# One shared semaphore and one wait for a last load and two partial sums, with other piece sizes in the last row

## The chip, the cores and the metric

The kernel runs on one core of a Trainium2 chip. The metric is the device time of the slowest core in microseconds (us); with one core there is only that. A profile also has a *span*, from the first instruction of the kernel to its last; the device time is longer.

The engines named in the profile are DVE (VectorE), ACT (ScalarE), POOL (GpSimd) and SP (SyncE, which issues all transfers here). SPq and DVEq are the instruction queues (sequencers) of SP and DVE.

## The reference

```python
def setup_inputs():
    batch, seq, dim = 32, 512, 1024
    return {"x": np.random.randn(batch, seq, dim).astype(np.float32)}

def reference(x):
    relu_x = np.maximum(x, 0)
    return np.sum(relu_x, axis=-1).astype(np.float32)
```

67 MB are read, 64 KB are written. Each of the 16,384 sums takes 1024 numbers.

## The kernel before

The rows are laid on 128 partitions, 128 rows to a partition. Seven chunks of 16 rows a partition (8 MB each) go through three buffers; then come loads of 8, 4, 2 and 1 rows, and a last row in three pieces. On the first six chunks ScalarE applies the relu to groups of rows and VectorE sums groups of rows; `ACT_STEPS` and `DVE_STEPS` are the groups. Afterwards both engines do relu and sum in one instruction, row by row.

```python
BIG = 16
ACT_STEPS = [[7, 9], [7, 9], [4, 5, 7], [4, 5, 7], [4, 5, 7], [3, 4, 5]]
DVE_STEPS = [[7, 9], [7, 4, 5], [4, 5, 7], [4, 5, 7], [4, 5, 7], [3, 4, 5]]
TAIL = [8, 4, 2, 1]
LAST = [512, 256, 256]
# ... (chunks: a buffer is refilled when VectorE has summed all of it)
    parts = [buf[:, tb, r, 0:n0], buf[:, tb, r, n0:n1], last[:, 0 : LAST[2]]]
    for k, (lo, hi) in enumerate([(0, n0), (n0, n1), (n1, D)]):
        sp.dma_start(out=parts[k], in_=xv[-1][:, BIG - 1, lo:hi]).then_inc(
            s_in[NBIG + len(TAIL) + k], 16
        )
# ... (the summing of a chunk)
        for n in DVE_STEPS[c]:
            if ready[r + n - 1] > seen:
                seen = ready[r + n - 1]
                dve.wait_ge(s_act, seen)
            dve.tensor_reduce(
                out=res[:, c * BIG + r : c * BIG + r + n],
                in_=buf[:, c % NB, r : r + n, :], axis=X, op=ALU.add,
            ).then_inc(s_dve, 1)
            r += n
# ... (the last row)
    n = LAST[2]
    act.wait_ge(s_in[-3], 16)
    on_act(parts[0], last[:, n : n + 1]).then_inc(s_part, 1)
    dve.wait_ge(s_in[-2], 16)
    on_dve(parts[1], last[:, n + 1 : n + 2]).then_inc(s_part, 1)
    dve.wait_ge(s_part, 2)
    dve.wait_ge(s_in[-1], 16)
    on_dve(last[:, :], res[:, J - 1 : J]).then_inc(s_tdve, 1)

    sp.wait_ge(s_tdve, 1)
    sp.dma_start(out=ov[-1][:, :], in_=res[:, start[-1] : J]).then_inc(s_out, 16)
```

The last row: ScalarE sums its first piece and VectorE its middle piece, and each writes its partial sum into one of two extra columns beside the last piece. VectorE's last instruction then sums the last piece and the two extra columns together (a partial sum of relus is never negative, so the relu does not touch it). That instruction therefore needs three things: the last load, ScalarE's partial, VectorE's own partial.

## Time and profile before

| | before |
|---|---|
| device time, median of 3 runs | 161.14 us (161.12 to 161.21) |
| span of the profile | 159.8 us |
| DMA queue 1, share of 16 engines' span | 98.0% |
| DVE busy, ACT busy | 121.4 us (76%), 101.5 us (64%) |
| landing of the last load to the end of the span | some 2.1 us |

The row to start from is the third: the transfers fill the span, and the engines fit beside them.

### The profile page before, as it was taken

How to read it: one execution, taken by the hardware profiler on the slowest of the kernel's cores; microseconds unless marked ns; L12 is line 12 of the kernel's file. 1: busy time of each engine (PE TensorE's matmuls, PEld its weight loads, DVE VectorE, ACT ScalarE, POOL GpSimd, SP SyncE). 2: the span in 40 equal slices, each digit the busy share in tenths (PEclk: the TensorE clock that was granted, in tenths of full speed). 3: DMA queues.
4: the chain of work that ended last, by engine and by line, in shares of the span. 5: the costliest groups of instructions: out<-in, count | busy, mean ns of one | idle time of the engine just before them, and what ended most of it. 6: DMA issues, size and time to landing. Idle time of an engine off the chain costs nothing.

```text
span 159.8 us, 149 instructions
## 1 busy us (share of the span) xinstructions
DVE 121.4 (76%) x58; ACT 101.5 (64%) x55; POOL 0.2 (0%) x4
## 2 busy tenths in 40 slices
DVE  0000000999959999999969989699899999598995
ACT  3000059990699708996099951999339980496974
POOL 0000000000000000000000000000000000000000
DMA  9979996996997998999979969969969969899993
GB/s 377 492 323 415 492 525 263 525 525 263 525 476 312 525 427 361 525 394 394 525 312 476 525 279 509 525 263 525 525 263 525 509 279 525 353 435 390 416 404 122
DMA packets 2449, 67.18 MB, mean 421 GB/s; under 512 B 528, under 2 KB 784, under 8 KB 1168
## 3 DMA queue, kind: packets, MB, share of 16 engines
q1 hardware_dynamic: 2448, 67.18, 98.0%
q14 instruction: 1, 0.01, 0.0%
HBM read 67.11 MB, written 0.07 MB: 420 GB/s over the span
## 4 chain that ended last, share of the span: by engine, by line
DMA 68%; ACT 18%; DVE 11%; SPq 1%; issue 0%
DMA buf<-in_x_dram 68%; ACT buf L133 18%; DVE res L148 11%; SPq L95 1%; SPq L103 0%; DVE last L118 0%; DVE buf L118 0%
## 5 line engine op out<-in xcount | busy, mean ns | idle before, releaser
L148 DVE TENSOR_REDUCE res<-buf 128x7 f32<-128x7168 f32 (+4 forms) x17 | 100.1, 5923 | 33.9 <-ACT buf L133 33.9
L133 ACT ACTIVATE buf<-buf 128x7168 f32<-128x7168 f32 (+4 forms) x16 | 80.7, 5099 | 46.0 <-DMA buf<-in_x_dram 46.0
L115 ACT ACTIVATE buf<-buf 128x1024 f32<-128x1024 f32 (+1 forms) x19 | 19.0, 1001 | 9.0 <-DMA buf<-in_x_dram 8.9
L118 DVE TENSOR_SCALAR_CACHE_REDUCE buf<-buf 128x1024 f32<-128x1024 f32 (+2 forms) x19 | 20.9, 1146 | 2.8 <-DMA buf<-in_x_dram 2.7
L115 ACT ACTIVATION_READ_ACCUMULATOR buf<-buf 128x1 f32 x19 | 3.5, 187 | 0.0
L133 ACT ACT_TABLE_LOAD x1 | 1.3, 1283 | 1.3 <-PEq L209 1.3
L118 DVE DVE_READ_ACCUMULATOR buf<-buf 128x1 f32 x19 | 1.6, 83 | 0.0
L118 DVE TENSOR_SCALAR_CACHE_REDUCE last<-last 128x258 f32<-128x258 f32 x1 | 0.4, 423 | 0.0
L178 DVE TENSOR_TENSOR res<-half 128x1 f32<-128x1 f32 x1 | 0.2, 160 | 0.1
L209 POOL MEMSET const-bfloat16-1.0<- 128x1 bf16 x1 | 0.1, 102 | 0.0
L209 POOL MEMSET const-uint8-127<- 128x1 uint8 x1 | 0.1, 101 | 0.0
L209 POOL MEMSET const-float32-0.0<- 128x1 f32 x1 | 0.1, 99 | 0.2 <-issue 0.2
L209 POOL MEMSET const-float32-1.0<- 128x1 f32 x1 | 0.1, 98 | 0.0
L118 DVE DVE_READ_ACCUMULATOR last<-last 128x1 f32 x1 | 0.1, 83 | 0.0
## 6 DMA issues: line engine op xcount, KB each, us to landing
buf<-in_x_dram SPq DMA_DIRECT2D x1, 7680.0 KB, 21.4
buf<-in_x_dram SPq DMA_DIRECT2D x1, 4096.0 KB, 26.7
buf<-in_x_dram SPq DMA_DIRECT2D x1, 2048.0 KB, 31.2
buf<-in_x_dram SPq DMA_DIRECT2D x2, 512.0 KB, 18.8
buf<-in_x_dram SPq DMA_DIRECT2D x1, 1024.0 KB, 33.2
buf<-in_x_dram SPq DMA_DIRECT2D x1, 256.0 KB, 34.2
buf<-in_x_dram SPq DMA_DIRECT2D x1, 128.0 KB, 34.1
last<-in_x_dram SPq DMA_DIRECT2D x1, 128.0 KB, 33.9
```

The lines of the kernel that those rows point to most:

```text
L95: sp.dma_start(out=buf[:, tb, r : r + n, :], in_=xv[-1][:, r : r + n, :]).then_inc(s_in[NBIG + i], 16)
L115: return act.activation(t, t, AF.Relu, accum_out=acc)
L118: return dve.tensor_scalar(out=t, in0=t, scalar1=0.0, scalar2=None, op0=ALU.max, op1=ALU.add, accum_out=acc)
L133: act.activation(t, t, AF.Relu).then_inc(s_act, 1)
L148: dve.tensor_reduce(out=res[:, c * BIG + r : c * BIG + r + n], in_=buf[:, c % NB, r : r + n, :], axis=X, op=ALU.add,).then_inc(s_dve, 1)
L178: dve.tensor_tensor(out=res[:, j0 + r : j0 + r + 1], in0=half[:, 0:1], in1=half[:, 1:2], op=ALU.add)
L209: nc = _bacc.Bacc("TRN2", target_bir_lowering=False, num_devices=1)
```

## The change

The load of the last piece no longer has a semaphore of its own. It counts on the one that the two partial sums count on, and VectorE's last instruction waits once, for 16 + 2 = 18. The pieces of the last row become 512, 224, 288, to make VectorE's own partial ready sooner. And VectorE's reduction of 9 rows in the first chunk is cut into 4 and 5.

```diff
-DVE_STEPS = [[7, 9], [7, 4, 5], [4, 5, 7], [4, 5, 7], [4, 5, 7], [3, 4, 5]]
+DVE_STEPS = [[7, 4, 5], [7, 4, 5], [4, 5, 7], [4, 5, 7], [4, 5, 7], [3, 4, 5]]
 TAIL = [8, 4, 2, 1]
-LAST = [512, 256, 256]
+LAST = [512, 224, 288]
@@
-    n_in = NBIG + len(TAIL) + len(LAST)
+    n_in = NBIG + len(TAIL) + len(LAST) - 1
@@
-            s_in[NBIG + len(TAIL) + k], 16
+            s_in[NBIG + len(TAIL) + k] if k < 2 else s_part, 16
@@
-    act.wait_ge(s_in[-3], 16)
+    act.wait_ge(s_in[-2], 16)
     on_act(parts[0], last[:, n : n + 1]).then_inc(s_part, 1)
-    dve.wait_ge(s_in[-2], 16)
+    dve.wait_ge(s_in[-1], 16)
     on_dve(parts[1], last[:, n + 1 : n + 2]).then_inc(s_part, 1)
-    dve.wait_ge(s_part, 2)
-    dve.wait_ge(s_in[-1], 16)
+    dve.wait_ge(s_part, 16 + 2)
     on_dve(last[:, :], res[:, J - 1 : J]).then_inc(s_tdve, 1)
```

## The prediction

> **What bounds the kernel now.** I read the page's slices first, then busy time by stretch, the chain of waits in order of time, the groups by shape, and last the timeline of the final two microseconds.
>
> The slices (tenths of busy time in 40 parts of the span):
>
> ```profile
> DVE  0000000999959999999969989699899999598995
> ACT  3000059990699708996099951999339980496974
> DMA  9979996996997998999979969969969969899993
> ```
>
> The DMA row is full from the first slice to the last but one, while VectorE (DVE) and ScalarE (ACT) have holes. Busy time by stretch, cut where each 8 MB chunk lands, which is 0.02 us ahead of ScalarE's first step on it in the timeline (length, DVE, ACT, POOL, clock, DMA share, GB/s):
>
> ```profile
> 41.15:60.50 19.35, 17.36 (x4) 13.95 (x2) 0.00 (x0) 1.00 1.00 434
> 60.50:79.85 19.35, 19.35 (x4) 14.04 (x3) 0.00 (x0) 1.00 1.00 434
> 99.20:118.55 19.35, 17.47 (x4) 14.04 (x3) 0.00 (x0) 1.00 1.00 434
> ```
>
> ScalarE starts on the chunks at 41.17, 60.52, 79.87, 99.22 and 118.57: always 19.35 us apart, at a DMA share of 1.00 in each stretch shown, so the transfers alone set the pace until the last byte is in. What a change of waits can move is only what follows the last bytes. The end of the chain of waits (start, us, what):
>
> ```profile
> 123.29 34.06 DMA buf<-in_x_dram
> 157.35 0.02 issue
> 157.37 0.32 DVE buf L118
> 157.69 0.03 issue
> 157.72 0.09 DVE buf L118
> 157.81 0.02 issue
> 157.84 0.43 DVE last L118 x2
> ```
>
> The middle piece of the last row lands at 157.35, VectorE sums it until 157.81, and the last piece starts at 157.84, straight behind VectorE's own work. When did that last piece land? The view of the tile "last" gives:
>
> ```profile
> L103 SPq DMA_DIRECT2D last<-in_x_dram x1: 447/447/447, 123.8 to 123.8; - x1
> DMA to landing us min/median/max: 33.9/33.9/33.9
> ```
>
> The timeline has this issue at 123.78, so it landed at 123.78 + 33.9 = 157.68, give or take 0.05 for rounding. The other arm is ScalarE's, in the timeline:
>
> ```profile
> 156.99 0.63 ACT L115 ACTIVATE buf<-buf 128x512 f32<-128x512 f32 x1
> 157.37 0.42 DVE L118 TENSOR_SCALAR_CACHE_REDUCE buf<-buf 128x256 f32<-128x256 f32 x1 [0.15 <-DMA buf<-in_x_dram]
> 157.53 0.19 ACT L115 ACTIVATION_READ_ACCUMULATOR buf<-buf 128x1 f32 x1
> 157.72 0.08 DVE L118 DVE_READ_ACCUMULATOR buf<-buf 128x1 f32 x1
> 157.84 0.42 DVE L118 TENSOR_SCALAR_CACHE_REDUCE last<-last 128x258 f32<-128x258 f32 x1
> 158.29 0.34 SPq L193 DMA_DIRECT2D out_dram<-res  x1
> ```
>
> ScalarE's partial is ready at 157.53 + 0.19 = 157.72. So three things must be there before the last instruction: the load at about 157.68, ScalarE's partial at 157.72, VectorE's own at 157.81. VectorE's own comes last. The last load has about 0.13 us of slack, the ScalarE arm 0.09 us.
>
> **What the Trainium skill says.** "DMA: Bandwidth & Descriptors", section "Why a DMA increments its semaphore by 16 and not by 1", says that each of up to 16 engines posts one increment, and that a semaphore shared by two transfers in flight can pass a wait too early. Here only one transfer shares its semaphore, with two single increments, and the wait asks for 18, the sum of all; it can pass only when all three are in. No run here has shown it yet; the result's correctness will. "Perfetto Trace Analysis", section "Identifying Dependency Chains", says that an instruction that waits on several engines may get an extra semaphore instruction ahead of it. That is what the change takes away. The trace of before shows no such row; the gap at this place is 0.03 us (157.81 to 157.84), and single waits show the same: the addition of the halves starts 0.03 us after ScalarE's half (156.84 + 0.19 = 157.03 to 157.06), the final store 0.03 us after VectorE's last read (158.18 + 0.08 = 158.26 to 158.29). The same page, section "Per-instruction lifecycle", says that a VectorE window runs from execution to write acknowledgement and leaves out waits and propagation; these 0.03 us gaps agree. The DMA page, section "How a descriptor splits into AXI transactions", says that a descriptor that doesn't start on 256 bytes also fetches from the boundary below. The last piece will start at column 736, byte 2944, which is 11.5 times 256. No run here shows its cost.
>
> **The change part by part.**
>
> (1) The first chunk's reduction of 9 rows becomes 4 + 5. The groups by shape (count, busy us, mean ns, idle before):
>
> ```profile
> L148 DVE TENSOR_REDUCE res<-buf 128x5 f32<-128x5120 f32 x5 | 27.4, 5482 | 0.0
> L148 DVE TENSOR_REDUCE res<-buf 128x4 f32<-128x4096 f32 x5 | 22.1, 4416 | 2.8 <-ACT buf L133 2.8
> L148 DVE TENSOR_REDUCE res<-buf 128x9 f32<-128x9216 f32 x1 | 9.8, 9753 | 0.2 <-ACT buf L133 0.2
> ```
>
> 4416 + 5482 - 9753 = 145 ns more. Both halves wait for the same ScalarE step, so nothing starts earlier. The reduction ends at 45.69 in place of 45.54. That frees the buffer of the fourth chunk, issued now at 45.57, but the third chunk is still streaming until 60.50: some 15 us of slack. VectorE itself idles 1.83 us after it, waiting for ScalarE (timeline, at 47.38). On the path: 0.
>
> (2) Middle piece 256 to 224 columns. Per column VectorE takes (686 - 420) / 256 = 1.04 ns, from the groups 128x512 (686 ns) and 128x256 (420 ns); 32 fewer are 33 ns. The piece also lands earlier: 32 x 4 x 128 = 16 KB less; at the 364 to 434 GB/s of the traces 38 to 45 ns, call it 0.04 us. Landing 157.31, start 157.33, accumulator read done 0.44 - 0.03 = 0.41 us later at 157.74 (was 157.81).
>
> (3) Last piece 256 to 288 columns, the instruction 258 to 290: 33 ns more. All bytes together are the same, so it lands as before at 157.68; if the misaligned start costs 128 bytes on each of 128 rows, that is another 16 KB, 0.04 us: 157.72.
>
> (4) One wait for 18 in place of two waits. The gaps above say 0.03 us either way: 0, at most some 0.02.
>
> Sum: the last instruction can start 0.03 us after the latest of VectorE 157.74, ScalarE 157.72 and the load 157.68 to 157.72, so at 157.77 in place of 157.84: 0.07 earlier. It takes 0.033 longer. VectorE ends, and the store starts, 0.04 us earlier. **161.14 - 0.04 = 161.10 us.** The change is a balancing act: three arms within 0.06 us of each other in place of 0.13.
>
> **The rivals.** (a) *The load becomes the bound.* The misaligned 1152-byte rows land later than thought, say 157.80: the start is then about where it was and the longer instruction makes it 0.03 slower, 161.17. For it: the landing is known to 0.05 only and the last microsecond moves 304 to 374 GB/s, not 434. Against it: 0.13 us of slack to eat.
> (b) *The waits were worth more than the gaps show.* If the second wait hid a decode, another 0.02 to 0.03 goes: 161.07. Against it: the gap after two waits equals that after one.
> (c) *The split reduction reaches the end.* If VectorE's 0.145 us were carried through, 161.25. Against it: the idle times above, and the DMA share of 1.00 in all the stretches between.
> (d) *The build itself moves the time*, through placement or start-up, by more than any of these. The three runs of before spread over 0.09 us (161.12 to 161.21), twice my effect; only this could carry it out of the range.
>
> **Range and chances.** Mechanisms alone give 161.05 to 161.20; run spread widens it to 161.00 to 161.25, which I take for 8 in 10. Two per cent would be 3.2 us, more than everything after the last byte (157.3 to 159.8), so faster or slower by that needs the stream itself to change, and no part touches it: 0.01 each, 0.98 for within 2%.
>
> **What would show it right or wrong.** Right: chunks still 19.35 us apart; the middle piece's reduction near 387 ns and the last near 456 ns; the gap ahead of the last instruction still about 0.03 us; the store issued 0.04 us sooner relative to the middle piece's old landing. From the middle piece's landing to the last instruction's start I expect 0.46 us (157.31 to 157.77), with the chain still running through the middle piece; a longer distance, and a chain that comes from the DMA of "last", would show rival (a). A gap under 0.02 us shows (b). A longer chunk spacing, or VectorE no longer idle ahead of the second chunk's first reduction, shows (c). I am wrong on the mechanism if the end moves while these rows do not, and wrong on the whole if the stream's rate changes.

## The result, and the profile after

The changed kernel took 161.22 us (median of 6 runs, 161.11 to 161.23), the kernel before 161.15 us in the same rounds (6 runs, 160.99 to 161.21). The ratio is 1.0004 with a 95% interval of 0.9991 to 1.0017: the same.

The slices of the changed kernel's page show the transfers as full as before:

```profile
DMA  9979996996996998989979969969969969899993
```

The busy time by stretch, again cut where the chunks land (start and end of the stretch, length, DVE, ACT, POOL, clock, DMA share, GB/s):

```profile
41.19:60.54 19.35, 17.43 (x4) 13.95 (x2) 0.00 (x0) 1.00 1.00 434
99.24:118.59 19.35, 17.47 (x4) 14.04 (x3) 0.00 (x0) 1.00 1.00 434
```

The stream is untouched: 19.35 us a chunk at 434 GB/s, only the whole of it 0.04 us later in this one execution. The cut reduction stands in the timeline (start, duration, engine, what it does, in brackets the idle time before it):

```profile
35.84 9.81 DVE L148 TENSOR_REDUCE res<-buf 128x4 f32<-128x4096 f32 x2 [0.15 <-ACT buf L133]
47.42 7.62 DVE L148 TENSOR_REDUCE res<-buf 128x7 f32<-128x7168 f32 x1 [1.76 <-ACT buf L133]
```

The two take 9.81 us together (9.75 for the one of before), and VectorE still idles 1.76 us after them (1.83 before). Then the end of the chain of waits of the changed kernel (start, us, what):

```profile
122.31 34.01 DMA buf<-in_x_dram
156.32 0.02 issue
156.35 1.41 ACT buf L115 x4
157.75 0.02 issue
157.77 0.47 DVE last L118 x2
```

It no longer passes through VectorE's middle piece but through ScalarE. The timeline shows why:

```profile
157.02 0.63 ACT L115 ACTIVATE buf<-buf 128x512 f32<-128x512 f32 x1
157.31 0.39 DVE L118 TENSOR_SCALAR_CACHE_REDUCE buf<-buf 128x224 f32<-128x224 f32 x1
157.56 0.19 ACT L115 ACTIVATION_READ_ACCUMULATOR buf<-buf 128x1 f32 x1
157.62 0.08 DVE L118 DVE_READ_ACCUMULATOR buf<-buf 128x1 f32 x1
157.77 0.46 DVE L118 TENSOR_SCALAR_CACHE_REDUCE last<-last 128x290 f32<-128x290 f32 x1
158.27 0.34 SPq L192 DMA_DIRECT2D out_dram<-res  x1
```

VectorE's partial is ready at 157.62 + 0.08 = 157.70, ScalarE's at 157.56 + 0.19 = 157.75, and the last instruction starts at 157.77 (before: 157.84). The groups by shape have the two resized instructions (count, busy us, mean ns, idle before):

```profile
L118 DVE TENSOR_SCALAR_CACHE_REDUCE last<-last 128x290 f32<-128x290 f32 x1 | 0.5, 456 | 0.1
L118 DVE TENSOR_SCALAR_CACHE_REDUCE buf<-buf 128x224 f32<-128x224 f32 x1 | 0.4, 386 | 0.1
```

The middle one fell from 420 to 386 ns, the last one rose from 423 to 456. The store is issued at 158.27 in place of 158.29. With the landings to the nanosecond, as the trace's semaphore records have them:

| ready, us from the span's start | before | after |
|---|---|---|
| first piece of the last row lands | 156.969 | 156.997 |
| middle piece lands | 157.349 | 157.287 |
| last piece lands | 157.644 | 157.661 |
| ScalarE's partial | 157.715 | 157.742 |
| VectorE's partial | 157.800 | 157.705 |
| last instruction starts | 157.835 | 157.774 |
| last instruction's sum is read out (end) | 158.265 | 158.239 |
| first piece's landing to that end | 1.296 | 1.242 |

So the tail behaves as planned: measured from the landing of the first piece, it is 0.054 us shorter. None of that is seen in the time, whose runs of one kernel already spread over 0.1 to 0.2 us. The span of both profiles is 159.8 us.

### The profile page after: what moved, and what is told of

It is laid out like the page before. It is cut to its first block, busy times and chain, and to the rows that moved or that the text cites. A ratio compares the mean times of both kernels' runs of the same rounds, so it can differ in the third digit from the quotient of the medians.

```text
span 159.8 us, 149 instructions
## 1 busy us (share of the span) xinstructions
DVE 121.5 (76%) x59; ACT 101.4 (63%) x55; POOL 0.2 (0%) x4
## 4 chain that ended last, share of the span: by engine, by line
DMA 68%; ACT 18%; DVE 11%; SPq 1%; issue 0%
DMA buf<-in_x_dram 68%; ACT buf L133 18%; DVE res L148 11%; ACT buf L115 1%; SPq L95 1%; DVE last L118 0%
## 5 line engine op out<-in xcount | busy, mean ns | idle before, releaser
L148 DVE TENSOR_REDUCE res<-buf 128x4 f32<-128x4096 f32 (+3 forms) x18 | 100.1, 5601 | 33.9 <-ACT buf L133 33.9
L118 DVE TENSOR_SCALAR_CACHE_REDUCE last<-last 128x290 f32<-128x290 f32 x1 | 0.5, 456 | 0.1
```

What stands on the lines that cost most here:

```text
L118: return dve.tensor_scalar(out=t, in0=t, scalar1=0.0, scalar2=None, op0=ALU.max, op1=ALU.add, accum_out=acc)
L148: dve.tensor_reduce(out=res[:, c * BIG + r : c * BIG + r + n], in_=buf[:, c % NB, r : r + n, :], axis=X, op=ALU.add,).then_inc(s_dve, 1)
```

## The experiments

Twelve kernels ran, all correct. They take the change apart, measure a wait by itself, and follow up one surprise. My theory was the prediction's: the sizes alone make the small gain, the removed wait and the cut reduction are worth nothing. The table has what all of them gave. Kernels are compared only within the same rounds. *VectorE* is the number of its records in the trace, separate wait instructions included. *Outside* is the time minus the span, over all runs of the kernel (spans are listed to 0.1 us, so a single value is good to 0.05). *Gap* is the time from the moment when the last of the three things was ready to the start of VectorE's last instruction. *Row* and *piece* are the distances from the landing of the 1-row load, and of the last row's first piece, to the end of VectorE's last instruction; the text calls the second one the tail, and it is left out where the first piece has another size. *VectorE*, *gap*, *row* and *piece* are read from one profiled execution of each run.

| run | us, median | before | ratio (95%) | VectorE | outside, us | gap, us | row, us | piece, us |
|---|---|---|---|---|---|---|---|---|
| before, first profile | 161.15 | | | 61 | | 0.035 | 1.982 | 1.296 |
| after, first profile | 161.22 | 161.15 | 1.0004 (0.9991 to 1.0017) | 61 | 1.31 to 1.36 | 0.032 | 1.916 | 1.242 |
| again_before | 161.16 | 161.03 | 1.0008 (0.9995 to 1.0020) | 61 | 1.33 to 1.40 | 0.035 | 1.983 | 1.263 |
| again_after | 161.24 | 161.03 | 1.0008 (0.9994 to 1.0022) | 61 | 1.32 to 1.36 | 0.032 | 1.915 | 1.240 |
| wait_only | 161.65 | 161.03 | 1.0036 (1.0023 to 1.0048) | 60 | 1.70 to 1.93 | 0.035 | 1.961 | 1.279 |
| sizes_only | 161.04 | 161.03 | 1.0002 (0.9989 to 1.0014) | 61 | 1.31 to 1.39 | 0.043 | 1.933 | 1.251 |
| steps_only | 161.16 | 161.13 | 1.0002 (0.9987 to 1.0017) | 62 | 1.34 to 1.38 | 0.034 | 1.979 | 1.277 |
| swap_waits | 161.18 | 161.13 | 1.0001 (0.9986 to 1.0016) | 61 | 1.31 to 1.40 | 0.131 | 2.053 | 1.353 |
| late_load_two | 161.48 | 161.13 | 1.0020 (1.0003 to 1.0037) | 61 | 1.32 to 1.40 | 0.120 | 2.243 | |
| late_load_one | 161.76 | 161.13 | 1.0034 (1.0020 to 1.0049) | 60 | 1.46 to 1.86 | 0.025 | 2.118 | |
| pad_vector | 161.19 | 161.13 | 1.0004 (0.9990 to 1.0017) | 61 | 1.30 to 1.40 | 0.035 | 1.925 | 1.266 |
| fewer_reduce | 161.78 | 161.13 | 1.0034 (1.0019 to 1.0048) | 60 | 1.60 to 1.99 | 0.035 | 1.966 | 1.274 |
| pad_scalar | 161.61 | 161.13 | 1.0027 (1.0015 to 1.0040) | 60 | 1.65 to 1.90 | 0.035 | 1.970 | 1.276 |
| balanced | 160.98 | 161.13 | 0.9991 (0.9979 to 1.0004) | 61 | 1.32 to 1.38 | 0.033 | 1.859 | |

For the kernel before, the outside time was 1.31 to 1.40 us in all 25 runs beside these.

### again_before and again_after: how far the same program moves

Edit: none, in both.

> The kernel before, unchanged, as a control of how far the same program's time and trace move. My theory (the extra 0.07 us that the six runs of the changed kernel showed is scatter): ratio 1.000 with an interval of about 0.001 either side, and the profile's tail, from the landing of the first piece of the last row to the end of VectorE's last instruction, at 1.30 us as in the first profile of before, within 0.02; the landing of that first piece itself may move by 0.05 or more. Rival (the two programs differ in time for good): the control's time stays within 0.02 of 161.15 and the changed kernel's stays above 161.20.

> The changed kernel, unchanged. My theory: the tail, from the landing of the first piece of the last row to the end of VectorE's last instruction, is 1.24 us again (1.30 before), within 0.02, with ScalarE's partial the last of the three to be ready; the whole time is within 0.1 us of the control, so the 0.05 us saved is there in the tail but drowns in where the stream ends and how long the store takes. Rival (the change slows something else): the time is above the control by 0.07 us or more again, and the extra shows in the landing of the first piece, later by that much than in the control.

Both gave a ratio of 1.0008 to the same runs of before, although one of them *is* the kernel before. By their letter both rivals' expectations came true (161.16 for the control, 161.24 for the changed kernel, and a later landing of the first piece), but the same program's two medians, 161.03 and 161.16, lie further apart than the 0.07 us in question. So the times do not tell the two apart. The tail does: 1.240 us again for the changed kernel. The control's tail came at 1.263 us, further from 1.30 than I had allowed; the first profile's 1.296 was the longest of the seven profiles with pieces 512, 256, 256 and no wait reordered (1.263 to 1.296, mean 1.276). The three with 512, 224, 288 have 1.240 to 1.251, mean 1.244. The gain of the tail is therefore 0.03 us, and the two groups do not overlap. Measured from the 1-row load the means differ by 0.05 us (1.967 and 1.921), but there one profile of the first group, pad_vector with 1.925, lies below one of the second, sizes_only with 1.933. The profiled run of again_after was its longest, 161.56 us; in it the first piece of the last row landed 0.44 us later than in the control (157.453 against 157.014), so in this run the extra time was in the stream, and its other runs went down to 161.04.

### wait_only: the shared semaphore alone

```diff
 (against the changed kernel)
-DVE_STEPS = [[7, 4, 5], [7, 4, 5], [4, 5, 7], ...
+DVE_STEPS = [[7, 9], [7, 4, 5], [4, 5, 7], ...
-LAST = [512, 224, 288]
+LAST = [512, 256, 256]
```

> Only the shared semaphore and the one wait for 18; pieces 512, 256, 256 and the first chunk's reduction as before. My theory: the removed wait was met about 0.1 us before VectorE's own partial, so removing it gives nothing: the gap from the end of VectorE's own accumulator read to the start of the last instruction is 0.035 us (0.03 to 0.04) as before, the tail 1.30 us within 0.02. Rival (the second wait cost a decode): the gap falls under 0.02 us and the tail is 0.02 to 0.05 shorter.

The gap was 0.035 us and the tail 1.279, so inside the span my theory held: the removed wait had been met at 157.67 in the first trace of before, 0.13 us ahead of VectorE's own partial. But the kernel was slower by 0.36%, with an interval that excludes 1, which neither theory had. Its span is 159.8 us like before's. The loss lies *outside* the span: time minus span is 1.70 to 1.93 us in place of 1.31 to 1.40. The profile page has a trace of it. This is the DMA queues' part of the page of before:

```profile
q1 hardware_dynamic: 2448, 67.18, 98.0%
q14 instruction: 1, 0.01, 0.0%
```

The same part of the page of wait_only has the first of these two rows alone. The one instruction fetch that fell into the span of before no longer does. Busy time by stretch around the end finds it again; the last number of a row is GB/s. First before, then wait_only:

```profile
159.50:160.20 0.70, 0.00 (x0) 0.00 (x0) 0.00 (x0) 1.00 0.03 12
160.20:162.00 1.80, 0.00 (x0) 0.00 (x0) 0.00 (x0) 1.00 0.00 0
```

```profile
159.50:160.20 0.70, 0.00 (x0) 0.00 (x0) 0.00 (x0) 1.00 0.00 0
160.20:162.00 1.80, 0.00 (x0) 0.00 (x0) 0.00 (x0) 1.00 0.02 9
```

In before, 12 GB/s for 0.7 us are some 8 KB at 159.5 to 160.2, beside the end of the final store. In wait_only nothing moves there, and some 16 KB come after 160.2, when the kernel's last instruction (159.77) is long over. To the nanosecond, the packet records have one fetch of 8192 bytes at 159.73 us in before, and two, at 161.08 and 161.39, in wait_only, the first 1.3 us after the span's end. From this I made a new theory: the removed wait was an instruction, and with one fewer on VectorE an instruction fetch comes too late to hide behind the final store.

### sizes_only: the pieces alone

```diff
 (against before)
-LAST = [512, 256, 256]
+LAST = [512, 224, 288]
```

> Only the pieces 512, 224, 288; two waits and the first chunk's reduction as before. My theory: the sizes alone make the whole gain: the last instruction starts 0.03 to 0.04 us after ScalarE's partial, VectorE's own partial being ready 0.03 us or more earlier, and the tail is 1.24 us within 0.02, as in the changed kernel. The last piece, which now starts off a multiple of 256 bytes, lands no later relative to the row before it than with 256 columns (1.36 us after the 1-row load's landing in before, 1.34 in the changed kernel). Rival (the extra wait instruction now lies in the way, as the load and ScalarE's partial come close together): the gap after ScalarE's partial is 0.05 us or more and the tail 1.26 or longer.

The sizes make the gain by themselves: tail 1.251 us, VectorE's partial ready 0.029 us before ScalarE's. The last piece landed 1.351 us after the 1-row load (before: 1.361), so its start off a multiple of 256 bytes cost nothing that can be seen. The rival has a small part in it: the last instruction started 0.043 us after ScalarE's partial, not 0.032, and a likely reason is the separate wait on the load, which ended at 157.660: the next instruction started 0.071 us later (157.731), the same distance that the next runs show.

### steps_only: the cut reduction alone

```diff
 (against before)
-DVE_STEPS = [[7, 9], [7, 4, 5], [4, 5, 7], ...
+DVE_STEPS = [[7, 4, 5], [7, 4, 5], [4, 5, 7], ...
```

> Only the first chunk's reduction of 9 rows cut into 4 and 5. My theory: it lengthens VectorE's work on the first chunk by 0.06 us (9.81 against 9.75 in the two traces), all of it taken from VectorE's idle time ahead of the second chunk (1.83 us, falling to about 1.77); chunks still land 19.35 us apart; tail 1.30 us, as before; time within 0.1 us of before. Rival (it is carried to the end): time up by 0.06 us with an interval that excludes zero, or a later landing of the fourth chunk.

As expected inside the span. In its timeline, VectorE's idle time ahead of the second chunk is 1.76 us, chunks land 19.35 us apart, and the time is that of before. The time alone could not tell (its interval allows some 0.27 us more); the idle time does. So the cut costs nothing that can be seen, and alone it gains nothing either: with 62 instructions in place of 61 the outside time stays at 1.34 to 1.38 us.

### swap_waits, late_load_two, late_load_one: what a separate wait costs

In the trace of before, one of the last two waits is carried by the summing instruction, and the other stands as an instruction of its own in front of it; the separate one is on the load, whose wait is written last. swap_waits writes the two in the other order, and its trace has the separate one on the partial sums, which come last:

```diff
 (against before)
-    dve.wait_ge(s_part, 2)
-    dve.wait_ge(s_in[-1], 16)
+    dve.wait_ge(s_in[-1], 16)
+    dve.wait_ge(s_part, 2)
```

> The kernel before with its last two waits written in the other order, so that the separate wait instruction is on the partial sums, which come last, and the summing instruction itself waits for the load. My theory: now the separate instruction lies on the path, as its wait is met last: it starts 0.03 us after VectorE's own partial, takes 0.02 us, and the summing instruction follows it, so the gap from VectorE's accumulator read to the last instruction is 0.07 to 0.11 us in place of 0.035. Rival (a separate wait is free wherever it stands): gap 0.035 us again.

The end of the chain of waits of swap_waits (start, us, what):

```profile
157.47 0.44 DVE buf L118 x2
157.91 0.03 issue
157.94 0.02 DVEq L188
157.96 0.07 issue
158.03 0.43 DVE last L118 x2
```

The separate wait (DVEq L188) is now a link of the chain: it starts 0.03 us after VectorE's partial, takes 0.02, and the instruction behind it starts 0.07 later. The gap is 0.131 us in place of 0.035. I had expected 0.07 to 0.11, having left most of those last 0.07 us out. The other way to expose the wait is to let the load come last; the second edit is late_load_two's with the changed kernel's shared semaphore:

```diff
 (late_load_two, against before; late_load_one, against wait_only)
-LAST = [512, 256, 256]
+LAST = [384, 128, 512]
```

> Pieces 384, 128, 512 with the two waits of before, so that the last load comes last of the three by some 0.19 us (estimate from the two traces) and the separate wait instruction, which is on the load, is met last. My theory: the start of the last instruction is 0.07 to 0.11 us after the load's landing. Rival (a separate wait is free): 0.02 to 0.04 us after it. The last instruction is longer by 256 columns, so its time is about 0.69 us and the whole tail is no better than before.

> Pieces 384, 128, 512 with the one wait for 18. The last load comes last by some 0.19 us. My theory: the last instruction starts 0.02 to 0.04 us after the load's landing, so the shared semaphore is worth 0.05 us against the same pieces with two waits, in a place where the wait is exposed. Rival (a wait is free): the same distance as with two waits. The time is within 0.3 us of before either way.

With two waits the last instruction started 0.120 us after the load's landing, with one wait 0.025 us after it. Where the wait is exposed, the shared semaphore is thus worth 0.095 us, twice what I expected. And yet late_load_one was the slower of the two, 161.76 against 161.48 us, both further from before (161.13) than the 0.3 us that I had allowed: it has 60 instructions on VectorE, and its outside time rose to 1.46 to 1.86 us. A point of reading on the side: three things count on one semaphore in late_load_one, and the profile puts the wait down to ScalarE, which had been ready at 157.53; the landing records say it was the load, at 157.68.

### pad_vector, fewer_reduce, pad_scalar: whose instructions count

pad_vector gives wait_only its lost instruction back, far from the end and from the shared semaphore:

```diff
 (against wait_only)
-DVE_STEPS = [..., [4, 5, 7], [3, 4, 5]]
+DVE_STEPS = [..., [4, 5, 7], [3, 4, 2, 3]]
```

> The one wait alone (pieces 512, 256, 256, first chunk's reduction of 9 rows whole), but with the last reduction of the sixth chunk, 5 rows, cut into 2 and 3, so that VectorE has as many instructions as in before. New theory, from the one-wait run: what counts is the number of VectorE's instructions; one fewer than in before moves an instruction fetch from beside the final store to after the span's end, and the time outside the span rises from 1.35 to 1.7 to 1.9 us. So here: time minus span 1.31 to 1.40, the fetch of 8192 bytes back at 1.1 to 1.4 us after VectorE's last instruction, time within 0.1 us of before. Rival (the shared semaphore itself costs it): time minus span 1.7 or more, time 161.5 or more.

fewer_reduce takes one of VectorE's instructions from the kernel before and leaves every wait and semaphore alone:

```diff
 (against before)
-DVE_STEPS = [[7, 9], [7, 4, 5], [4, 5, 7], ...
+DVE_STEPS = [[7, 9], [7, 9], [4, 5, 7], ...
```

> The kernel before with the second chunk's reductions 4 and 5 joined into one of 9, so that VectorE has one instruction fewer; all waits and semaphores as before. New theory (the number of VectorE's instructions): time minus span 1.6 to 1.9 us in place of 1.35, the last instruction fetch after the span's end, time 161.4 or more, though VectorE has 0.06 us less to do. Rival (the shared semaphore): time and time minus span as before.

pad_scalar gives wait_only an instruction back, but on ScalarE:

```diff
 (against wait_only)
-ACT_STEPS = [[7, 9], [7, 9], ...
+ACT_STEPS = [[7, 4, 5], [7, 9], ...
```

> The one wait alone, with ScalarE's first step of 9 rows cut into 4 and 5: the program has as many instructions in all as before, VectorE one fewer. New theory (VectorE's own number counts): time minus span stays at 1.6 to 1.9 us, time 161.4 or more. Rival (the size of the whole program counts): 1.35 us and time as before.

Busy time by stretch of pad_vector, then of fewer_reduce, as it was shown for before and wait_only:

```profile
159.40:160.20 0.80, 0.00 (x0) 0.00 (x0) 0.00 (x0) 1.00 0.03 10
160.20:162.00 1.80, 0.00 (x0) 0.00 (x0) 0.00 (x0) 1.00 0.02 5
```

All three came out as the new theory had it. pad_vector is back at 161.19 us with 1.30 to 1.40 us outside, and its fetch of 8192 bytes is back at 159.50, 1.31 us after VectorE's last instruction. fewer_reduce lost 0.34% without any change to a semaphore, and pad_scalar stayed slow. In the last two the fetch is at 161.02 and 161.06 us, 1.32 us after the span's end in each. So it is VectorE's own number of instructions that counts: 61 or 62 leave 1.3 to 1.4 us outside the span, 60 leave 1.5 to 2.0. Other numbers were not tried.

Does the program's end wait for the late fetch? The records of the four profiled executions with 60 instructions say that the two go together. A fetch is over when its start and its duration have passed; all times here are counted from the end of the span:

| run | last fetch over, us | time outside, us | difference, us |
|---|---|---|---|
| fewer_reduce | 1.831 | 1.600 | 0.231 |
| pad_scalar | 1.829 | 1.604 | 0.225 |
| wait_only | 1.969 | 1.734 | 0.235 |
| late_load_one | 2.079 | 1.845 | 0.234 |

The outside time differs by 0.25 us among them and follows the end of the last fetch to 0.01. (Why the difference is 0.23 us and not zero, the records do not say.) That the end waits for the fetch is the plain reading; a delay common to both is not excluded. In the other ten profiles the fetch is over between 0.02 us before and 0.75 us after the span's end, and the time outside is 1.34 to 1.36 whatever it does. One thing more moves with the number: after the span the trace records five groups of semaphore updates, each in rising order of the semaphores' numbers; the group 156 to 206 begins 0.85 us after the span's end with 60 instructions and 0.30 to 0.32 with 61 or 62, while the other four begin at the same places in all profiles, to 0.01 us. This is before the recorded fetch starts, so that fetch is not its reason. What makes the fetch late, and why the border lies between 60 and 61, stays open.

### balanced: pieces that bring the three in together

```diff
 (against the changed kernel)
-LAST = [512, 224, 288]
+LAST = [480, 224, 320]
```

> The changed kernel with pieces 480, 224, 320, meant to let ScalarE's partial, VectorE's partial and the load come in together. Estimate from the traces: ScalarE's work 32 columns shorter (27 ns), all of it starting 0.04 us earlier against the end of the stream, the last instruction 33 ns longer: from the landing of the 1-row load to the end of VectorE's last instruction 1.88 us, against 1.92 in the changed kernel and 1.98 in before; the load is then the last or equal last of the three. Time within 0.1 us of before and of the changed kernel: too little to be seen in it. Rival (the stream's end moves with the sizes): that distance 1.92 or more.

The timeline of balanced:

```profile
157.35 0.19 ACT L115 ACTIVATION_READ_ACCUMULATOR buf<-buf 128x1 f32 x1
157.45 0.08 DVE L118 DVE_READ_ACCUMULATOR buf<-buf 128x1 f32 x1
157.57 0.49 DVE L118 TENSOR_SCALAR_CACHE_REDUCE last<-last 128x322 f32<-128x322 f32 x1
```

The load is in at 157.513, VectorE's partial at 157.530 and ScalarE's at 157.533: all within 0.02 us, and the instruction starts at 157.57. From the 1-row load's landing to the end it is 1.859 us, 0.056 less than in the changed kernel (1.915), where I had expected 1.88. ScalarE, not the load, is last by a hair. With 160.98 us it has the lowest median of all, but its ratio of 0.9991 has an interval that includes 1, so that it beats both kernels is seen in the tail, of one profile, and not in the time.

## Why the prediction was right or wrong, point by point

The number held: 161.22 us lies in the range of 161.00 to 161.25, and "the same" was right. The working held inside the span, and missed a pair of terms outside it. That these two cancelled was luck: with the waits joined and the reduction of 9 rows left whole, as in wait_only (with the old pieces), the time was 161.65 us, outside the range.

- **What bounds the kernel.** Right. The chunks stayed 19.35 us apart in both kernels and in every experiment whose chunks I read; nothing in the change reached the stream.
- **Part 1, the cut reduction.** Right that it costs nothing on the path. The size was off: 145 ns were a sum of three durations, but two reductions back to back overlap, and together they took 9.81 us in the timeline, 0.06 more than the one.
- **Part 2, the middle piece.** Right in mechanism. The reduction took 386 ns (387 predicted). The landing was mis-sized: against the 1-row load it came about 0.1 us sooner (0.964 us in the changed kernel, 1.066 before), not 0.04. VectorE's partial was ready at 157.705, not 157.74, so ScalarE's at 157.742 became the last of the three. I had named VectorE.
- **Part 3, the last piece.** Right: 456 ns, as predicted. The possible cost of the odd start was not seen (1.351 us in sizes_only, 1.338 in the changed kernel, 1.361 in before).
- **Part 4, the waits.** Right that the gap stays at 0.03 us (0.035, then 0.032): the removed wait had been met early. One reading was wrong: I had said that the trace of before shows no extra semaphore instruction. The views that I had read leave such instructions out; the trace's records have one on VectorE (L188, 157.671 to 157.692). The runs add that its cost was a matter of place. In sizes_only the gap was 0.011 us longer than with one wait, and where the wait is met last, 0.095.
- **The sum inside the span.** The start at 157.77 was met (157.774). The predicted gain of 0.04 us measures 0.054 between the first two profiles and 0.03 between the means of the groups, from the first piece's landing (0.05 from the 1-row load's).
- **The term that was missing.** "On the path: 0" for part 1 and "0, at most some 0.02" for part 4 were each wrong for the time as a whole. Taking one instruction from VectorE costs some 0.45 us outside the span (wait_only 1.82 us on the mean of its runs, against 1.34 for before's in that call; fewer_reduce 1.83 and pad_scalar 1.81, against 1.37 in theirs); putting one back took it off again in pad_vector (1.36 on the mean). In the changed kernel the joined wait takes one away and the cut reduction puts one back, and they cancel. I had counted what each instruction takes and not how many there are. Rival (d), a build that moves the time by more than any of the parts, came nearest, though I had looked for it at the start and not at the end.
- **The other rivals.** (a) did not happen: the load stayed 0.08 us ahead of ScalarE. (b) was refuted with the old sizes. (c) was refuted by the idle time in steps_only.

What stays open is whether the changed kernel's time is 0.03 us below before's, as its tail says: the runs of one program scatter by more than ten times that. Open, too, is what makes the fetch late with 60 instructions.

## What to carry to other kernels

When three inputs meet in one instruction, write down when each is ready and size the work so that they come in together; here a second wait cost nothing while it was met early, and some 0.1 us when it was met last, so the separate wait belongs on what comes first (in both orders tried, the wait written last became the separate one). Look at the time minus the span as well as at the span: an edit that only changes how many instructions an engine has moved the time by 0.45 us here, where the profile's engines showed nothing. Before crediting or blaming an edit, try the same number of instructions without it.

## What the Trainium skill lacked or had wrong

- "Runtime: NRT & Kernel Launch", section "Instruction fetch mechanics", says that instructions are fetched autonomously in blocks of 16 KiB and that the cost of crossing a block boundary is "mostly hidden". At the end of a program it need not be: with 60 instead of 61 or 62 instructions on VectorE the last fetch starts at 161.0 to 161.6 us in place of 159.4 to 160.0, and the time outside the span, which in the four profiles follows the end of that fetch, is 1.46 to 1.99 us in place of 1.30 to 1.40. The packets here are of 8192 bytes, one or two of them recorded at the end. The section says nothing of fetches at a program's end.
- "Perfetto Trace Analysis", section "Identifying Dependency Chains", says that an extra semaphore instruction may be inserted where an instruction waits on several engines, but gives no cost. Here it takes 0.02 us, and the instruction behind it starts 0.07 us later; met last, it adds 0.095 us, and met early, nothing.
- "DMA: Bandwidth & Descriptors", section "Rules for kernel authors", asks for a semaphore of its own for a DMA and for waits on multiples of 16. A wait for 18, on a semaphore shared by one transfer and two engine increments, gave correct results in all six kernels that used it. The rule says nothing of a wait for the sum of all increments; that it is safe in general is not shown by these runs.
- The same page, section "How a descriptor splits into AXI transactions", has descriptors that start off a multiple of 256 bytes fetch more. No cost was seen here: rows of 1152 bytes that start at byte 2944 landed 1.29 to 1.35 us after the 1-row load, those of 1024 bytes on the boundary 1.32 to 1.38.
